# A two-layer hybrid block on one core: a fourth Strassen group per layer, with another sum, another order of the adding transfers, earlier bank copies and moved condition sums

## The chip, the cores and the metric

The kernel runs on one core of a Trainium2 chip. The metric is the device time in microseconds (us). The kernel before was run three times: 1801.11, 1798.59 and 1798.97 us, so its median is 1798.97 us. A further execution was profiled: it took 1799.28 us, and its recorded span, from the first to the last instruction, is 1797.2 us.

## The reference

Two layers are applied to one sequence of 512 tokens of width 1024, all in float32. Each layer has a mixing half (three attention-like branches, gated) and a convolutional feed-forward half. Both are preceded by an RMS norm whose scale and shift come from a condition vector. What matters here is the condition and the feed-forward half:

```
mod = silu(c) @ w_ada + b_ada                      # [6144] per layer
shift1, scale1, gate1, shift2, scale2, gate2 = jnp.split(mod, 6, axis=-1)
...                                                # mixing half, updates x
h2 = modulate(rms_norm(x, norm2_g), shift2, scale2)
u, g = jnp.split(h2 @ w_up, 2, axis=-1)            # w_up: 1024 x 5632, so u and g are 512 x 2816
u = causal_dwconv(u, w_conv, b_conv)               # 3 taps along the sequence
y = (jax.nn.silu(u) * g) @ w_down                  # 2816 x 1024
x = x + gate2 * y
```

## The kernel before, in words

**Weights.** The host cuts all weight matrices into 128x1024 float32 tiles (512 KB) in the order of use. Matrix work goes by *units*: one unit uses one such tile. A tile is loaded from DRAM by a transfer on SyncE's queue (`dma_to`) into one of six buffers (`wr`, `NR = 6`). ScalarE rounds it to the matmul's format (`prep_hi`, line 194, the tile `wh`), and VectorE subtracts that to get the rest (`prep_lo`, line 203, the tile `wl`). `wh` and `wl` have five buffers each. Activations are split in the same way (`hhi`, `hlo`), and every product is three matmuls: wh·hhi, wh·hlo, wl·hhi.

**Feed-forward up-projection.** `w_up` gives 22 columns (blocks of 128) of u and 22 of g, and column j of both is needed together. Per layer, columns 0 to 2 are made in `head_group`, beside the norm. Columns 3 to `J0 - 1` are made one after the other by `col_block`: one unit is one block of 24 matmuls over 512 tokens, first u, then g. Columns from `J0` on are made in *Strassen groups* of four columns (`ff_group`; with `NG = 3` groups, `J0` is 10).

**A group.** The four u columns and four g columns and the eight 128-wide slices of the input make a 2x2 by 2x2 block product over half the tokens each. It takes seven block products instead of eight. Each is two units of 24 matmuls over 256 tokens, so a group has 14 units. Four of the seven weight operands are sums of weight tiles. They are made before use by *adding transfers*: GpSimd issues a DMA that adds a tile from DRAM onto a tile that is in a buffer (`acc_to`, line 186). `_plan` lists the units, with "r" for a raw tile and the tile that is added to it, if any. In the order of products the operands are a11; a21+a22; a12; that sum + a11; a11+a21; the sum of the fourth product + a12; a22. `accs` is the list of adding transfers; `acc_to` takes them strictly from its front, and only when the buffer's earlier use is past.

The products accumulate in PSUM banks (bA, bB, bC, two halves t = 0 and 1). Between two products a bank's state is copied out or combined: `e1`, `e5`, `u2` (line 1175) and `c21` are copies by ScalarE, `c11`, `c22`, `c12` are sums by VectorE. `at(n, ...)` files such a step under the group's n-th unit. At each unit, `prod` first prepares the tiles of units ahead (`prep_lo` to the third unit, `prep_hi` to the fourth), and then issues the steps filed there. `u2` must be done before the fifth product goes on in bank bA.

**Sums of the input.** Four of the seven activation operands are sums too: per slice k, `t_sum` makes two sums (ta, tb) and rounds them, `t_low` makes the rests. They are issued one by one between the plain blocks (list `TS`).

**Condition sums.** `mod` is made on VectorE: a row block of `w_ada` (512 KB) is loaded by SyncE's queue into one of the six weight buffers (`ada_dma`, line 225) and multiplied with the condition and summed up in one instruction (`ada_sum`, line 230). There are 80 of these. Every second `tick`, of which each plain block has two, does one of them while `ada_on` is set; `ada_need` does what is still missing when a section is needed. While such jobs are left, `dma_to` keeps one weight buffer back.

Each engine and each queue works in the order of issue, which is the order of this program.

Of the kernel before, what the change touches and what calls it, by code (L numbers as in the profile page):

```python
# [53 lines left out]
NG = 3  # L54
# [8 lines left out]
def _plan():  # L63
# [28 lines left out]
def tile_hybrid_layers(ctx: ExitStack, tc: tile.TileContext, xT, cvec, wall, wada, par, a2, cst, tabs, out):  # L92
# [105 lines left out]
    def prep_lo(u):  # L198
        while state["lo"] < min(u, NU):
# [4 lines left out]
            wgt[i] = (hi, lo)  # L204
            state["lo"] += 1
# [238 lines left out]
    def head_group(l, sec, nm, h, half):  # L444
# [42 lines left out]
        else:  # L487
# [77 lines left out]
    def layer(l, nm, h):  # L565
# [517 lines left out]
        due = {}  # L1083
        acts = [None] * KFF
# [10 lines left out]
        def t_sum(k):  # L1095
            ta, tb = slot("ta"), slot("tb")
            c, d = tks.pop((l, k)), tks.pop((l, k + 4))
# [7 lines left out]
            ah, bh = slot("tah", F32R), slot("tbh", F32R)  # L1105
            A.copy(ah[:, H0], ta[:, H0])
            A.activation(ah[:, H1], ta[:, H1], AF.Identity, bias=tabd[:, 4 + k:5 + k])
            A.copy(bh, tb)
            tmid[k] = ta, tb, ah, bh

        def t_low(k):
            ta, tb, ah, bh = tmid.pop(k)
            al, bl = slot("tal", F32R), slot("tbl", F32R)
            V.tensor_tensor(al[:, H0], ta[:, H0], ah[:, H0].bitcast(F32), op=ALU.subtract)
            V.scalar_tensor_tensor(out=al[:, H1], in0=ta[:, H1], scalar=tabd[:, 4 + k:5 + k],
                                   in1=ah[:, H1].bitcast(F32), op0=ALU.add, op1=ALU.subtract)
            V.tensor_tensor(bl, tb, bh.bitcast(F32), op=ALU.subtract)
            tt[k, 1], tt[k, 2] = (ah, al, 0), (ah, al, 256)
# [435 lines left out]
```

## Time and profile before

| | us |
|---|---|
| median of 3 runs | 1798.97 |
| the profiled execution | 1799.28 |
| its span | 1797.2 |
| TensorE busy with matmuls | 1771.0 (99%) |
| VectorE busy | 1084.3 (60%) |
| ScalarE busy | 741.2 (41%) |
| GpSimd busy | 147.1 (8%) |
| layer 0: 14 plain blocks, from 577.36 | 76.17 |
| layer 0: three groups, 653.53 to 794.71 | 141.18 |
| layer 1: 14 plain blocks, from 1476.10 | 76.17 |
| layer 1: three groups, 1552.27 to 1673.22 | 120.95 |

Matmuls are pipelined, so the time of a stretch is read from the start of one matmul to the start of another, not from the durations. The last four rows are such distances; a plain block is thus 76.17/14 = 5.44 us, and a unit of a group in layer 1 is 120.95/42 = 2.88 us.

### The profile page before, as it was taken

What the parts mean: (1) busy time and instruction counts of PE and PEld (TensorE: products, weight loads), DVE (VectorE), ACT (ScalarE), POOL (GpSimd) and SP (SyncE); (2) the same over time, 40 slices, a digit from 0 to 9 for tenths busy, and PEclk for the clock granted to TensorE, in tenths of its full rate; (3) what the DMA queues carried; (4) which work ended last, traced back from release to release, by engine and by line L of the source; (5) the groups of instructions that cost most, each with busy time, mean ns of one, the idle gap of its engine ahead of it and who ended that gap; (6) DMA issues with size and microseconds to landing.
All of it is one profiled execution on the core that took longest, in us unless ns stands there. A gap on an engine that the chain in (4) does not pass through costs nothing.

```text
span 1797.2 us, 24309 instructions
## 1 busy us (share of the span) xinstructions
PE 1771.0 (99%) x9601; PEld 1518.8 (85%) x9601; DVE 1084.3 (60%) x1639; ACT 741.2 (41%) x1233; POOL 147.1 (8%) x191
## 2 busy tenths in 40 slices
PE   8999999999999989999999999999999999999999
PEld 6888778888888879988898887788888888999887
DVE  7767654565666766675555576545644467466731
ACT  3674433432324335563236544334323244355610
POOL 3221100000010011100001111000000100111000
PEclk9999999999999999999999999999999999999999
DMA  9342223456553468774622422334552334587431
GB/s 366 124 135 66 71 95 110 145 174 227 182 174 101 150 192 199 191 243 146 243 90 94 133 67 71 96 130 145 163 182 94 109 115 117 119 221 191 163 111 42
DMA packets 78510, 259.99 MB, mean 145 GB/s; under 512 B 9096, under 2 KB 9522, under 8 KB 78396
## 3 DMA queue, kind: packets, MB, share of 16 engines
q1 hardware_dynamic: 68748, 224.86, 36.8%
q0 software_dynamic: 9648, 33.58, 9.0%
q8 instruction: 75, 1.23, 0.3%
q14 instruction: 39, 0.32, 0.1%
HBM read 250.00 MB, written 8.40 MB: 144 GB/s over the span
## 4 chain that ended last, share of the span: by engine, by line
PE 82%; DVE 9%; DMA 3%; ACT 3%; issue 2%; SPq 0%; POOL 0%; ACTq 0%; DVEq 0%; POOLq 0%
PE bm L320 17%; PE bm L322 17%; PE bm L321 17%; PE bm L459 4%; PE ga L459 4%; PE bm L627 3%; PE bm L628 3%; PE bm L629 3%; PE bm L1158 3%; PE bm L1160 2%; PE bm L1161 2%; DMA wr<-wall 2%; ACT wh L194 1%; PE ba L1161 1%; PE ba L1160 1%
## 5 line engine op out<-in xcount | busy, mean ns | idle before, releaser
L203 DVE TENSOR_TENSOR wl<-wr,wh 128x1024 fp32r<-128x1024 f32 x338 | 412.3, 1223 | 293.1 <-ACT wh L194 292.1
L194 ACT CAST wh<-wr 128x1024 fp32r<-128x1024 f32 x338 | 351.2, 1046 | 286.2 <-PE bm L321 130.0
L320 PE MATMUL bm<-hhi,wh 128*128 128x512 f32 x912 | 366.1, 401 | 0.0
L322 PE MATMUL bm<-hhi,wl 128*128 128x512 f32 x912 | 355.7, 390 | 0.0
L321 PE MATMUL bm<-hlo,wh 128*128 128x512 f32 x912 | 355.5, 390 | 0.0
L320 PEld LDWEIGHTS bm<-hhi,wh 128*128 128x128 f32 x912 | 171.3, 188 | 37.1 <-issue 2.8
L322 PEld LDWEIGHTS bm<-hhi,wl 128*128 128x128 f32 x912 | 171.2, 188 | 36.8
L321 PEld LDWEIGHTS bm<-hlo,wh 128*128 128x128 f32 x912 | 171.5, 188 | 35.9 <-issue 1.4
L320 PE MATMUL bm<-fah,wh 128*128 128x512 f32 (+1 forms) x374 | 141.0, 377 | 0.0
L321 PE MATMUL bm<-fal,wh 128*128 128x512 f32 (+1 forms) x374 | 140.8, 377 | 0.0
L322 PE MATMUL bm<-fah,wl 128*128 128x512 f32 (+1 forms) x374 | 140.8, 377 | 0.0
L230 DVE SCALAR_TENSOR_TENSOR ar<-ar,cact 128x1024 f32<-128x1024 f32 x80 | 97.4, 1219 | 8.5 <-DMA ar<-wada 8.5
L627 PE MATMUL bm<-wh,hhi 128*128 128x512 f32 (+1 forms) x256 | 96.1, 376 | 0.0
L628 PE MATMUL bm<-wl,hhi 128*128 128x512 f32 (+1 forms) x256 | 93.5, 365 | 0.0
L629 PE MATMUL bm<-wh,hlo 128*128 128x512 f32 (+1 forms) x256 | 93.3, 365 | 0.0
L322 PEld LDWEIGHTS bm<-fah,wl 128*128 128x128 f32 x374 | 70.4, 188 | 13.0
L320 PEld LDWEIGHTS bm<-fah,wh 128*128 128x128 f32 x374 | 70.4, 188 | 12.8
L321 PEld LDWEIGHTS bm<-fal,wh 128*128 128x128 f32 x374 | 70.4, 188 | 12.7
L1022 DVE SCALAR_TENSOR_TENSOR x<-bm,mod,x 128x512 f32<-128x512 f32 (+1 forms) x39 | 25.3, 654 | 80.6 <-PE bm L322 80.5
L186 POOL DMA_DIRECT2D wr<-wall x48 | 41.7, 986 | 378.6 <-DVE wl L203 217.2
L985 ACT ACTIVATE mg<-bm,der 128x512 f32<-128x512 f32 x48 | 32.9, 685 | 73.7 <-PE bm L322 73.7
L1158 PE MATMUL bm<-tbh,wh 128*128 128x256 f32 x192 | 56.0, 292 | 6.4 <-ACT uu L1175 6.4
(288 smaller groups left out, 3431.5 us busy)
## 6 DMA issues: line engine op xcount, KB each, us to landing
wr<-wall SPq DMA_DIRECT2D x302, 512.0 KB, 3.6
ar<-wada SPq DMA_DIRECT2D x80, 512.0 KB, 4.2
wr<-wall POOLq DMA_DIRECT2D x48, 512.0 KB, 9.2
ad<-wada SPq DMA_DIRECT2D x32, 256.0 KB, 6.1
x<-xT SPq DMA_DIRECT2D x16, 256.0 KB, 4.8
x<-xm SPq DMA_DIRECT2D x16, 256.0 KB, 6.6
xm<-x POOLq DMA_DIRECT2D x10, 256.0 KB, 3.3
cumb<-cumd POOLq DMA_DIRECT2D x8, 256.0 KB, 6.3
```

What stands on the lines that cost most here:

```text
L194: A.copy(hi, raw[plan[i][1]])
L203: V.tensor_tensor(lo, raw[plan[i][1]], hi.bitcast(F32), op=ALU.subtract)
L230: V.scalar_tensor_tensor(out=r, in0=r, scalar=1.0, in1=cact, op0=ALU.mult, op1=ALU.mult, accum_out=mod[l][:, b:b + 1])
L320: T.matmul(o, lhsT=wh, rhs=ah, start=first, stop=False)
L321: T.matmul(o, lhsT=wh, rhs=al, start=False, stop=False)
L322: T.matmul(o, lhsT=wl, rhs=ah, start=False, stop=last)
L459: T.matmul(banks[f % GB][:, ts], lhsT=got[f // 8][wi][:, (f % 8) * 128:(f % 8) * 128 + 128], rhs=h[kc][hi][:, ts], start=kc == 0 and hf != ...
L627: T.matmul(o, lhsT=h[k][0][:, bs], rhs=wh[:, ws], start=k == 0, stop=False)
L628: T.matmul(o, lhsT=h[k][0][:, bs], rhs=wl[:, ws], start=False, stop=False)
L629: T.matmul(o, lhsT=h[k][1][:, bs], rhs=wh[:, ws], start=False, stop=k == KD - 1)
L1158: T.matmul(o, lhsT=wh[:, sl], rhs=ah, start=first and i == 0 and k == 0, stop=False, skip_group_check=True)
L1160: T.matmul(o, lhsT=wh[:, sl], rhs=al, start=False, stop=False, skip_group_check=True)
```

## The change

- `NG` is 4, so `J0` is 6: per layer, eight plain blocks are replaced by a fourth group of 14 units.
- The sixth product's operand (the sum of the fourth product + a12) is made by VectorE: when the fourth product's tile has been split, one instruction adds it onto a12 in a12's buffer ("v" in the plan). Three pairs of adding transfers per group are left of four.
- The list of adding transfers is sorted by when the buffer that they add to was last used.
- In `prod`, the steps that free or combine banks come first in a unit (`first_at`), ahead of the preparation, and `wl` is prepared one unit earlier, as far ahead as `wh`.
- `t_sum` and `t_low` are each cut in two (ta, tb). Five of the pieces move into `head_group`, two into the first group, and the others stay between the plain blocks, up to two behind each.
- No condition sums run between the plain blocks: `ada_on` is cleared before them and not after.

```diff
-NG = 3
+NG = 4
...
-        for dst, src in ((a11, None), (a21, a22), (a12, None), (a21, a11), (a11, a21), (a21, a12), (a22, None)):
+        for op, dst, src in (("r", a11, a11), ("r", a21, a22), ("r", a12, a12), ("r", a21, a11), ("r", a11, a21),
+                             ("v", a12, a21), ("r", a22, a22)):
             for i in range(2):
-                v.append(("r", dst[i], None if src is None else src[i]))
+                v.append((op, dst[i], src[i] if src != dst else None))
...
+    sums = {}
     for i, t in enumerate(plan):
-        if t[2] is not None:
+        if t[0] == "v":
+            sums[last[t[2]]] = t[1], t[2]
+        elif t[2] is not None:
             accs.append((i, t[1], t[2], last.get(t[1], -1)))
         endv[t[1]] = last[t[1]] = i
+    accs.sort(key=lambda a: a[3] if a[3] >= 0 else a[0] - 6.5)
...
             V.tensor_tensor(lo, raw[plan[i][1]], hi.bitcast(F32), op=ALU.subtract)
             wgt[i] = (hi, lo)
+            if i in sums:
+                d, a = sums[i]
+                V.tensor_tensor(raw[d], raw[d], raw[a], op=ALU.add)
...
+                for f in extra.get(kc, ()) if extra else ():
+                    f()
...
-        TS = [lambda: t_sum(0), lambda: t_low(0), lambda: t_sum(1), lambda: t_low(1),
-              lambda: t_sum(2), lambda: t_low(2), lambda: t_sum(3), lambda: t_low(3)]
+        TS = [lambda k=k, f=f: f(k) for k, f in ((0, ta_sum), (1, ta_sum), (0, ta_low), (2, ta_sum), (1, ta_low),
+                                                 (3, ta_sum), (2, ta_low), (0, tb_sum), (3, ta_low), (1, tb_sum),
+                                                 (0, tb_low), (2, tb_sum), (1, tb_low), (3, tb_sum))]
+        TL = [lambda k=k, f=f: f(k) for k, f in ((2, tb_low), (3, tb_low))]
+        ex = {kc: [TS.pop(0)] for kc in range(3, KD)}
...
                 for t in range(2):
-                    prep_lo(cur[0] + 3)
-                    prep_hi(cur[0] + 4)
+                    for f in early.pop(cur[0], []):
+                        f()
+                    prep_to(cur[0] + 4)
                     dma_to(cur[0] + 12, True)
...
+            for n in range(len(TL)):
+                at(1 + n, TL.pop(0))
             for t in range(2):
-                at(1 + t, e1, t)
-                at(3 + t, e5, t)
-                at(5 + t, c11, t)
-                at(7 + t, u2, t)
-                at(9 + t, c22, t)
-                at(11 + t, c12, t)
-                at(13 + t, c21, t)
+                first_at(1 + t, e1, t)
+                first_at(3 + t, e5, t)
+                first_at(5 + t, c11, t)
+                first_at(7 + t, u2, t)
+                first_at(9 + t, c22, t)
+                first_at(11 + t, c12, t)
+                first_at(13 + t, c21, t)
...
+        ada_on[0] = False
+        while ada_raw:
+            i, b, post, r = ada_raw.pop(0)
+            ada_sum(i, b, r)
+            if post:
+                post()
         free(NA)
         far[0] = 6
         for j in range(3, J0):
...
             col_block(h2, pu_evac)
-            if TS:
-                TS.pop(0)()
+            for f in TS[:2]:
+                f()
+            del TS[:2]
             col_block(h2, pg_evac)
-            if TS:
-                TS.pop(0)()
-        ada_on[0] = False
+            for f in TS[:2]:
+                f()
+            del TS[:2]
         far[0] = 12
-        while ada_raw:
-            i, b, post, r = ada_raw.pop(0)
-            ada_sum(i, b, r)
-            if post:
-                post()
```

Three places show how the instructions move. In the listings a name's number is the tile's, L is the line in the kernel that the listing is of, so line 203 before is line 208 now, 1065 to 1077 are 1075 to 1087, 1175 is 1202, and 186 is 191.

**VectorE between the plain blocks, layer 0, before.** `wl` is the rest of a weight tile, `fu` the convolution's taps and the gate of one column, `ar` a condition sum, `ta` and `tb` the input sums.

```order
L203 TENSOR_TENSOR wl_5126<-wr_4934,wh_5124 128x1024
L1065 SCALAR_TENSOR_TENSOR fu_5143<-bm_5039,par0_85,fu_5143 128x511
L1067 SCALAR_TENSOR_TENSOR fu_5143<-bm_5039,par0_85,fu_5143 128x510
L1077 TENSOR_TENSOR fu_5143<-fu_5143,bm_5091 128x512
L230 SCALAR_TENSOR_TENSOR ar_5117,mod1_88<-ar_5117,cact_93 128x1024
L1098 TENSOR_TENSOR ta_5164<-ht_4641 128x256
L1099 SCALAR_TENSOR_TENSOR ta_5164<-ht_4813,ta_5164 128x256
L1101 SCALAR_TENSOR_TENSOR tb_5165<-ht_4813,tabd_4629,ht_4641 128x256
L1103 TENSOR_TENSOR tb_5165<-ht_4813 128x256
L1104 TENSOR_TENSOR tb_5165<-tb_5165,ta_5164 128x256
L203 TENSOR_TENSOR wl_5178<-wr_4998,wh_5176 128x1024
L230 SCALAR_TENSOR_TENSOR ar_5162,mod1_88<-ar_5162,cact_93 128x1024
```

The same place now:

```order
L208 TENSOR_TENSOR wl_5061<-wr_4955,wh_5059 128x1024
L1075 SCALAR_TENSOR_TENSOR fu_5078<-bm_4965,par0_85,fu_5078 128x511
L1077 SCALAR_TENSOR_TENSOR fu_5078<-bm_4965,par0_85,fu_5078 128x510
L1087 TENSOR_TENSOR fu_5078<-fu_5078,bm_5025 128x512
L1128 SCALAR_TENSOR_TENSOR tb_5096<-ht_4791,tabd_4629,ht_4638 128x256
L1130 TENSOR_TENSOR tb_5096<-ht_4791 128x256
L1131 TENSOR_TENSOR tb_5096<-tb_5096,ta_4847 128x256
L1138 TENSOR_TENSOR tbl_5102<-tb_5050,tbh_5051 128x512
L208 TENSOR_TENSOR wl_5106<-wr_4961,wh_5104 128x1024
```

The condition sums are gone from between the blocks, and a piece that needs ScalarE's rounding (`tbl`) now stands behind the sums of the next slice.

**ScalarE around `u2` in the first group, before.** `wh` is a rounded weight tile; `wr_5272` and `wr_5312` hold the operand of the sixth product here, the one that the fourth adding transfer makes.

```order
L194 CAST wh_5671<-wr_5312 128x1024
L1169 COPY gg_5673<-ba_5538 128x2x256
L194 CAST wh_5702<-wr_5353 128x1024
L194 CAST wh_5731<-wr_5387 128x1024
L194 CAST wh_5763<-wr_5272 128x1024
L1175 COPY uu_5578<-bm_5535 128x2x256
L194 CAST wh_5795<-wr_5312 128x1024
L1175 COPY uu_5610<-bm_5536 128x2x256
```

The same place now; the sixth product's operand is in `wr_5023` and `wr_5063`, a12's buffers:

```order
L199 CAST wh_5354<-wr_4959 128x1024
L199 CAST wh_5386<-wr_4961 128x1024
L199 CAST wh_5417<-wr_4963 128x1024
L1202 COPY uu_5255<-bm_5220 128x2x256
L199 CAST wh_5449<-wr_5023 128x1024
L1202 COPY uu_5287<-bm_5221 128x2x256
L199 CAST wh_5481<-wr_5063 128x1024
```

`u2` has moved ahead of the rounding of the sixth product's tiles, and those tiles no longer come from a transfer.

**GpSimd's adding transfers of the first group, before**, from the second pair on: a21 += a11 twice, a11 += a21 twice, a21 += a12 twice. The names in brackets are the counters that GpSimd waits on: DMASW those of earlier adding transfers, DMAHW those of loads, DVE and Activation those of VectorE and ScalarE.

```order
L186 DMA wr_5272<-wall 128x1024 [waits DMASW2_49,DMASW0_49,DVE_49]
L186 DMA wr_5312<-wall 128x1024 [waits DMASW3_49,DMASW1_49,DVE_49]
L186 DMA wr_5353<-wall 128x1024 [waits DMAHW4_49,DMAHW5_49,DMAHW1_49,DMASW4_49]
L186 DMA wr_5387<-wall 128x1024 [waits DMAHW6_49,DMAHW5_49,DMASW5_49]
L186 DMA wr_5272<-wall 128x1024 [waits DMASW6_49,DMASW2_49,DVE_49]
L186 DMA wr_5312<-wall 128x1024 [waits DMASW7_49,DMASW3_49,DVE_49]
```

The first group's transfers now, from the first pair on (a21 += a22, a11 += a21, a21 += a11):

```order
L191 DMA wr_4957<-wall 128x1024 [waits DMAHW4_49,DMAHW1_49,DMAHW5_49,DMAHW0_49,DMAHW7_49,DMASW0_49,DVE_49]
L191 DMA wr_4959<-wall 128x1024 [waits DMAHW2_49,DMAHW5_49,DMAHW0_49,DMAHW6_49,DMASW1_49,DVE_49]
L191 DMA wr_4961<-wall 128x1024 [waits DMAHW3_49,DMASW2_49,DVE_49]
L191 DMA wr_4963<-wall 128x1024 [waits DMAHW4_49,DMAHW6_49,DMASW3_49,DVE_49]
L191 DMA wr_4957<-wall 128x1024 [waits DMASW4_49,DMASW0_49,DVE_49]
L191 DMA wr_4959<-wall 128x1024 [waits DMASW5_49,DMASW1_49,DVE_49]
```

And VectorE now at the end of the fourth product's tiles (`wr_4957`, `wr_4959`), with the two new sums:

```order
L208 TENSOR_TENSOR wl_5323<-wr_4957,wh_5321 128x1024
L212 TENSOR_TENSOR wr_5023<-wr_5023,wr_4957 128x1024
L208 TENSOR_TENSOR wl_5356<-wr_4959,wh_5354 128x1024
L212 TENSOR_TENSOR wr_5063<-wr_5063,wr_4959 128x1024
L1199 TENSOR_TENSOR uu_5255<-uu_5255,bm_5224 128x2x256
```

The sum for a11 now stands ahead of the second sum for a21, and the fourth pair of transfers has become two VectorE instructions ahead of `c11` (line 1199).

By the order of issue, the 80 condition sums fall as follows. Before: 34 in layer 0 ahead of the feed-forward half, 15 between its plain blocks, 13 in its down-projection, 18 in layer 1's mixing half. Now: 34, 1 (ahead of the plain blocks), 13 and 32.

More of the change, by code (lines that the diff above doesn't have):

```diff
@@ L442, in ada0_sum, with head_group @@
         ada0_fin(kc, i, ada0_part(kc, i), E)
-    def head_group(l, sec, nm, h, half):
+    def head_group(l, sec, nm, h, half, extra=()):
         live[0] += NA
@@ L1083, in layer @@
         due = {}
+        early = {}
         acts = [None] * KFF
@@ L1093, in layer, with ta_sum @@
         tmid = {}
[L1095 to L1097 removed]
+        def ta_sum(k):
+            ta, ah = slot("ta"), slot("tah", F32R)
+            c, d = tks[l, k], tks[l, k + 4]
             V.tensor_tensor(ta[:, H0], c[:, H0], c[:, H1], op=ALU.subtract)
@@ L1100, in t_sum, with ta_low, tb_sum @@
                                    op1=ALU.subtract)
+            A.copy(ah[:, H0], ta[:, H0])
+            A.activation(ah[:, H1], ta[:, H1], AF.Identity, bias=tabd[:, 4 + k:5 + k])
+            tmid[k] = ta, ah
+        def ta_low(k):
+            ta, ah = tmid[k]
+            al = slot("tal", F32R)
+            V.tensor_tensor(al[:, H0], ta[:, H0], ah[:, H0].bitcast(F32), op=ALU.subtract)
+            V.scalar_tensor_tensor(out=al[:, H1], in0=ta[:, H1], scalar=tabd[:, 4 + k:5 + k],
+                                   in1=ah[:, H1].bitcast(F32), op0=ALU.add, op1=ALU.subtract)
+            tt[k, 1], tt[k, 2] = (ah, al, 0), (ah, al, 256)
+        def tb_sum(k):
+            tb, bh = slot("tb"), slot("tbh", F32R)
+            ta, _ = tmid[k]
+            c, d = tks.pop((l, k)), tks.pop((l, k + 4))
             V.scalar_tensor_tensor(out=tb[:, H0], in0=d[:, H1], scalar=tabd[:, k:k + 1], in1=c[:, H1], op0=ALU.add,
@@ L1104, in t_sum, with tb_low @@
             V.tensor_tensor(tb[:, H1], tb[:, H1], ta[:, H0], op=ALU.add)
-            ah, bh = slot("tah", F32R), slot("tbh", F32R)
-            A.copy(ah[:, H0], ta[:, H0])
-            A.activation(ah[:, H1], ta[:, H1], AF.Identity, bias=tabd[:, 4 + k:5 + k])
             A.copy(bh, tb)
[L1109 to L1116, printed above, removed]
+            tmid[k] = tb, bh
+        def tb_low(k):
+            tb, bh = tmid.pop(k)
+            bl = slot("tbl", F32R)
             V.tensor_tensor(bl, tb, bh.bitcast(F32), op=ALU.subtract)
-            tt[k, 1], tt[k, 2] = (ah, al, 0), (ah, al, 256)
             tt[k, 3], tt[k, 4] = (bh, bl, 0), (bh, bl, 256)
-        TS = [lambda: t_sum(0), lambda: t_low(0), lambda: t_sum(1), lambda: t_low(1),
-              lambda: t_sum(2), lambda: t_low(2), lambda: t_sum(3), lambda: t_low(3)]
+        TS = [lambda k=k, f=f: f(k) for k, f in ((0, ta_sum), (1, ta_sum), (0, ta_low), (2, ta_sum), (1, ta_low),
[3 more added lines that the diff above has]
+        ex = {kc: [TS.pop(0)] for kc in range(3, KD)}
         def ff_group(j0):
@@ L1142, in at, with first_at @@
                 due.setdefault(base + n, []).append(lambda: f(*a))
+            def first_at(n, f, *a):
+                early.setdefault(base + n, []).append(lambda: f(*a))
             def prod(banks, key, first):
                 for t in range(2):
-                    prep_lo(cur[0] + 3)
-                    prep_hi(cur[0] + 4)
+                    for f in early.pop(cur[0], []):
+                        f()
+                    prep_to(cur[0] + 4)
                     dma_to(cur[0] + 12, True)
@@ L1231, in ff_group @@
             free(3)
-        fb = head_group(l, 3, nm2, h2, True)
+        fb = head_group(l, 3, nm2, h2, True, ex)
         ahead()
@@ L1265, in layer @@
         tt.clear()
+        for n, fs in early.items():
+            due[n] = fs + due.get(n, [])
+        early.clear()
         rest = [f for n in sorted(due) for f in due[n]]
```

## The prediction

> **What bounds the kernel now.** I read the page first, then the busy table of the feed-forward stretches of both layers, then TensorE's waits.
>
> ```profile
> span 1797.2 us, 24309 instructions
> PE 1771.0 (99%) x9601; PEld 1518.8 (85%) x9601; DVE 1084.3 (60%) x1639; ACT 741.2 (41%) x1233; POOL 147.1 (8%) x191
> ```
>
> TensorE is busy throughout; the others have room on average. So time is won only by fewer or faster matmuls, or from the few places where TensorE stands. These are the plain blocks and the three groups of layer 0, then the same of layer 1:
>
> ```profile
> core 0: us, PE busy (x) PEld busy (x) DVE busy (x) ACT busy (x) POOL busy (x), PEclk, DMA share, GB/s
> 577.36:653.53 76.17, 76.17 (x338) 63.08 (x336) 55.70 (x90) 29.29 (x41) 1.83 (x2) 1.00 0.49 154
> 653.53:794.71 141.18, 129.24 (x1009) 127.84 (x1008) 92.27 (x109) 72.12 (x95) 19.13 (x22) 0.94 0.78 200
> 1476.10:1552.27 76.17, 76.17 (x338) 63.06 (x336) 48.99 (x74) 33.43 (x47) 2.65 (x3) 1.00 0.35 94
> 1552.27:1673.22 120.95, 120.95 (x1009) 120.95 (x1008) 81.25 (x92) 68.95 (x89) 18.06 (x21) 1.00 0.81 204
> ```
>
> The reader is to see that the same 1008 matmuls take 141.18 us in layer 0 and 120.95 us in layer 1, where TensorE never stands and its granted clock is 1.00. Layer 0 loses 20.23 us. TensorE's waits with a line of the groups are these (us in total, times, longest), and all seven lie in layer 0:
>
> ```profile
> PE bm L1158 <- ACT uu L1175: 6.4, 4, 3.4
> PE bm L1158 <- DVE fu L1067: 3.0, 1, 3.0
> PE ba L1158 <- ACT wh L194: 1.8, 1, 1.8
> PE ba L1161 <- DVE wl L203: 0.8, 1, 0.8
> ```
>
> That is 12.0 us of standing. The rest is the clock, 0.94 on the mean. After the longest wait the matmuls come every 0.2136 us (22 of them from the first to the second row here) instead of 120.95/1008 = 0.1200:
>
> ```profile
> 691.03 0.41 PE L1161 MATMUL bm<-tbh,wl 128*128 128x256 f32 x1
> 695.73 0.41 PE L1158 MATMUL bm<-tbh,wh 128*128 128x256 f32 x1
> ```
>
> A mean of 0.94 over 141.18 us means 16.9 us at half clock; each such microsecond does 0.1200/0.2136 of the work, so 7.4 us are lost. 12.0 + 7.4 = 19.4 of the 20.23; restarts are the remainder.
>
> Two causes show. First, `u2` (line 1175) stands on ScalarE behind a rounding that waits for an adding transfer, and TensorE waits for `u2`:
>
> ```profile
> 688.86 1.04 ACT L194 CAST wh<-wr 128x1024 fp32r<-128x1024 f32 x1 [2.95 <-DMA wr<-wall]
> 689.81 0.58 ACT L1175 COPY uu<-bm 128x512 f32<-128x512 f32 x1
> 690.44 0.58 PE L1158 MATMUL bm<-tbh,wh 128*128 128x256 f32 x1 [3.43 <-ACT uu L1175]
> ```
>
> By the order of issue that rounding is the sixth product's tile, the fourth adding transfer. Second, condition loads (line 225) stand in SyncE's queue, and each holds a weight buffer. Four of them come in a row just as layer 0's groups start, and the next two weight loads, a12 of the first group by the order of issue, start 10.8 us and more into the group; in layer 1 the second of the same pair started 22.6 us ahead of it:
>
> ```profile
> 651.89 5.29 SPq L225 DMA_DIRECT2D ar<-wada  x3
> 662.02 0.33 SPq L225 DMA_DIRECT2D ar<-wada  x1
> 664.30 2.74 SPq L180 DMA_DIRECT2D wr<-wall  x2
> 1529.65 0.33 SPq L180 DMA_DIRECT2D wr<-wall  x1
> ```
>
> Layer 1 runs the same code without condition sums there, so it is a control for that half of the change.
>
> **The change, part by part.**
>
> *Fourth group.* Per layer eight plain blocks go, 8/14 x 76.17 = 43.53 us, and a group comes at layer 1's pace, 120.95/3 = 40.32 us: a gain of 3.21 us per layer, 6.42 in all. Seven products instead of eight would give an eighth, 5.4 us; the row gives less, because a 256-token matmul takes 0.1200 us and not half of 76.17/336 = 0.2267. [...] The trace says 0.1200 and 0.2267, so the 3.21 stands.
>
> The six added units per layer cost ScalarE and VectorE a split each:
>
> ```profile
> L203 DVE TENSOR_TENSOR wl<-wr,wh 128x1024 fp32r<-128x1024 f32 x338 | 412.3, 1223 | 293.1 <-ACT wh L194 292.1
> L194 ACT CAST wh<-wr 128x1024 fp32r<-128x1024 f32 x338 | 351.2, 1046 | 286.2 <-PE bm L321 130.0
> L186 POOL DMA_DIRECT2D wr<-wall x48 | 41.7, 986 | 378.6 <-DVE wl L203 217.2
> L230 DVE SCALAR_TENSOR_TENSOR ar<-ar,cact 128x1024 f32<-128x1024 f32 x80 | 97.4, 1219 | 8.5 <-DMA ar<-wada 8.5
> ```
>
> 12 x 1.22 = 14.7 us of VectorE and 12 x 1.05 = 12.6 of ScalarE, beside TensorE: in layer 1's groups VectorE is busy 81.25 of 120.95 and ScalarE 68.95. On the path: nothing. If the cover goes, the late tile's 1.05 + 1.22 us show at once.
>
> *Sum by VectorE.* 16 instructions of the shape of line 203 (two SBUF operands, 128x1024): 16 x 1.22 = 19.6 us of VectorE. A group's VectorE work goes from 81.25/3 = 27.1 to 29.5 us, of 40.32: hidden. Behind each sum wait the next rests and `c11`; a unit is 2.88 us and the rests run three units ahead, so 1.22 us late is covered. GpSimd's transfers stay 48 (eight groups of six), so its 41.7 us stay; per group it is a quarter less, and the weight bytes per unit fall from 16 tiles in 14 units to 14 in 14.
>
> *Bank copies first.* `u2` no longer follows the sixth product's rounding, and that tile comes from VectorE. What is left behind `u2` is that rounding: it waits for `u2`, which waits for the fourth product, but is wanted only three units, 8.6 us, later. This takes out the 6.4 us and its clock.
>
> *Order of the adding transfers.* The a11 transfer no longer stands behind a21's second one, which waits for later rests. From issue to use one takes about 7.0 us (GpSimd's start of one in layer 1 to the rounding that ended its wait on it):
>
> ```profile
> 1561.30 0.85 POOL L186 DMA_DIRECT2D wr<-wall  x1 [4.06 <-DVE wl L203]
> 1568.34 1.05 ACT L194 CAST wh<-wr 128x1024 fp32r<-128x1024 f32 x1 [1.93 <-DMA wr<-wall]
> ```
>
> The rests are now made three units ahead, so a21's second transfer starts some five units, 14 us, ahead of its use: no cost, and the 1.93 us wait should shrink. A gain only off the path.
>
> *No condition sums beside the plain blocks.* 14 of layer 0's sums move into layer 1's mixing half, which then carries 32. Whether that costs is shown by the two mixing halves now (VectorE's condition sums, two records each, then all engines):
>
> ```profile
> 288.00:577.36 289.36, 41.68 (x68) 1.00 0.49 166
> 1186.74:1476.10 289.36, 20.84 (x34) 1.00 0.42 139
> 288.00:577.36 289.36, 289.32 (x1470) 246.64 (x1469) 173.24 (x271) 98.99 (x183) 11.49 (x17) 1.00 0.49 166
> 1186.74:1476.10 289.36, 289.34 (x1470) 246.63 (x1469) 153.78 (x236) 98.96 (x183) 11.49 (x17) 1.00 0.42 139
> ```
>
> 34 sums in layer 0 and 17 in layer 1 take the same 289.36 us. So 32 cost nothing. In layer 0's down-projection 13 remain, as before, and 34 + 1 + 13 = 48 is just what is wanted by then (32 of layer 0, 16 of layer 1's shift and scale): no spare one, but none missing.
>
> *Six plain blocks instead of fourteen, and the moved input sums.* Here the cover shrinks, and this is where I look for a loss. In layer 1 ScalarE and VectorE run behind TensorE after `head_group` and need about 10.2 us per column (pair of blocks, 10.88 us of TensorE), gate to gate:
>
> ```profile
> 1495.69 0.69 DVE L1077 TENSOR_TENSOR fu<-fu,bm 128x512 f32<-128x512 f32 x1 [0.76 <-ACT fu L1071]
> 1515.45 0.63 ACT L1071 ACTIVATE fu<-fu 128x512 f32<-128x512 f32 x1 [3.64 <-DVE fu L1067]
> 1516.12 0.69 DVE L1077 TENSOR_TENSOR fu<-fu,bm 128x512 f32<-128x512 f32 x1 [0.76 <-ACT fu L1071]
> ```
>
> The last two rows are the third column, the last plain one now. Its silu starts at 1515.45, while the groups would start at 1476.10 + 6 x 5.44 = 1508.74. The group's fourth tile is split behind that silu: 1515.45 + 0.63, then 1.05 and 1.22, ready at 1518.4. TensorE wants its rest at 1508.74 + 3 x 2.88 + 2 x 0.12 = 1517.6. So the upper bound is 0.8 us per layer. The lower bound: the new order gives each column one slice's input sums as now, but with ScalarE's rounding further ahead of its use; a wait of VectorE for ScalarE of up to 1 us per column falls away, and the tile is 2 us early. I take zero, since nearly all of the interval lies there.
>
> **The sum.** 1799.28 (the profiled execution) - 20.23 - 6.42 = 1772.63 us. That execution is 0.31 us above the median of the three, less than their spread, so I give 1772.6 for the median.
>
> **Rivals.**
>
> *Short stalls of the first groups.* If the fourth tile is late by 0.8 us and the input sums shift a few more, each layer pays 1 to 3 us, plus clock. [...]
>
> With half clock for as much as one of the two causes had (7.4/2 = 3.7) each layer pays up to 6: 1775 to 1785.
>
> *The first group is late for want of plain blocks, not for the condition loads.* Then only `u2`'s part of layer 0 is won, and both layers pay 3.0 + 1.8 + 0.8 = 5.6 us and, by their share of the first 9.0 us of waits, 4.6 of clock: 1772.6 + 2 x 10.2 = 1793. Against it: layer 1's third column is done when 0.8 us are missing at most, and a12's second load started 22.6 us early there.
>
> *VectorE becomes the bound, and the kernel slower.* The sum, `c11` and the rests stand in one queue; if `c11`, now ahead of the rests, waits for its bank while tiles three units on are wanted, every group stalls. One wait as the longest seen, 3.43 us, with half of the 7.4 us of clock, in each of eight groups: 1772.6 + 8 x 7.1 = 1829. It is slower only from (26.65 + 3.6)/8 = 3.8 us per group on. Against it: 29.5 of 40.32 us.
>
> *The moved sums show after all,* 14 x 1.22 = 17.1 us in layer 1's mixing half: 1790. Against it: the equal 289.36.
>
> **Chances.** The sum 0.68, short stalls 0.16, the late first group 0.08, moved sums 0.02, VectorE 0.04, and 0.02 for losses that just cancel the gain. 0.2% is 3.6 us and about what can be told from no change; faster by more: 0.68 + 0.16 + 0.08 + 0.02 = 0.94, within 0.02, slower 0.04. For 8 in 10 the range takes the sum and the short stalls: from 1770 (2.6 us under the sum, about the spread of the runs) to 1784.
>
> **What would show it.** Right: the two stretches from the first plain block to the last group's end are 6 x 5.44 + 56 x 2.88 = 193.9 us in each layer, with clock 1.00; no wait of line 1158's successor on `u2`; no condition sum between the plain blocks and 32 in layer 1's mixing half, still 289.4 us long; fewer and shorter waits of ScalarE's rounding on transfers. Wrong: a wait on `wl` or `wh` in the first three units of the first group, a clock below 1.00 behind it, or waits on `c11` in every group.

## The result, and the profile after

| | before | after |
|---|---|---|
| median, us (range, runs) | 1799.25 (1798.59 to 1801.11, 4) | 1772.85 (1772.09 to 1773.08, 4) |
| the profiled execution, us | 1799.28 | 1772.72 |
| ratio of the times | | 0.9851, 95% interval 0.9834 to 0.9868 |
| layer 0: plain blocks + groups, us | 76.17 + 141.18 = 217.35 | 32.64 + 161.27 = 193.91 |
| layer 1: the same | 76.17 + 120.95 = 197.12 | 32.64 + 161.27 = 193.91 |

The change saves 26.40 us on the medians and 26.56 between the two profiled executions. The two stretches account for it: 217.35 - 193.91 = 23.44 in layer 0 and 197.12 - 193.91 = 3.21 in layer 1, 26.65 in all.

The head of the page after, and the busy table of the stretches (layer 0's plain blocks and groups, then layer 1's):

```profile
span 1770.9 us, 24972 instructions
...
PE 1757.4 (99%) x9889; PEld 1521.2 (86%) x9889; DVE 1123.2 (63%) x1679; ACT 759.6 (43%) x1261; POOL 147.2 (8%) x191
```

```profile
core 0: us, PE busy (x) PEld busy (x) DVE busy (x) ACT busy (x) POOL busy (x), PEclk, DMA share, GB/s
577.71:610.35 32.64, 32.64 (x145) 27.03 (x144) 23.45 (x39) 13.71 (x19) 2.66 (x4) 1.00 0.55 123
610.35:771.62 161.27, 161.27 (x1345) 161.26 (x1344) 122.25 (x136) 93.82 (x122) 17.27 (x20) 1.00 0.70 178
1453.03:1485.67 32.64, 32.64 (x145) 27.03 (x144) 23.47 (x39) 13.70 (x19) 1.69 (x2) 1.00 0.48 107
1485.67:1646.94 161.27, 161.27 (x1345) 161.27 (x1344) 122.25 (x136) 93.81 (x122) 17.07 (x20) 1.00 0.70 178
```

Layer 0 and layer 1 are now alike to 0.01 us, TensorE is busy in all of both and its clock is 1.00. 161.27/4 = 40.32 us is the pace of a group that layer 1 had before. The list of TensorE's waits has no line of the groups any more (the first of its six; the others are 2.4 us and less, all from outside the groups):

```profile
PE fT L771 <- DVE st L839: 2.5, 2, 1.3
...
```

The weight tiles' groups of instructions, to be held against lines 203 and 194 before, and the new sums:

```profile
L208 DVE TENSOR_TENSOR wl<-wr,wh 128x1024 fp32r<-128x1024 f32 x350 | 426.5, 1223 | 274.0 <-ACT wh L199 273.3 <-DMA wr<-wall 0.2
L199 ACT CAST wh<-wr 128x1024 fp32r<-128x1024 f32 x350 | 362.8, 1047 | 221.2 <-PE bm L329 121.3 <-DMA wr<-wall 52.2 <-issue 38.9
...
L212 DVE TENSOR_TENSOR wr<-wr 128x1024 f32<-128x1024 f32 x16 | 19.5, 1219 | 0.0
```

Twelve more splits and 16 sums of 1.22 us. ScalarE's rounding waits 52.2 us for weight transfers in all, where the list of ScalarE's waits before has 84.7.

The place where the prediction looked for a loss is the first group of layer 0. These rows are ScalarE's third silu and its rounding of the group's fourth tile, VectorE's rest of that tile, and TensorE's first matmul with it:

```profile
614.86 0.63 ACT L1081 ACTIVATE fu<-fu 128x512 f32<-128x512 f32 x1 [2.12 <-DVE fu L1077]
615.39 1.03 ACT L199 CAST wh<-wr 128x1024 fp32r<-128x1024 f32 x1
616.46 1.23 DVE L208 TENSOR_TENSOR wl<-wr,wh 128x1024 fp32r<-128x1024 f32 x1 [0.25 <-ACT wh L199]
619.22 0.28 PE L1188 MATMUL ba<-tah,wl 128*128 128x256 f32 x1
```

The rest is done at 616.46 + 1.23 = 617.69, 1.53 us before TensorE takes it. The mixing half of layer 1 with its moved condition sums is as long as before: from the last group of layer 0 to the first plain block of layer 1 it is 1453.03 - 771.62 = 681.41 us, and it was 1476.10 - 794.71 = 681.39.

```profile
1163.67:1453.03 289.36, 38.00 (x62) 1.00 0.49 164
```

That row is VectorE's condition sums in the 289.36 us ahead of layer 1's plain blocks: 31 of them (two records each) where 17 stood, and TensorE does not show it.

### The profile page after: what moved, and what is told of

It is laid out like the page before. It is cut to its first block, busy times and chain, and to the rows that moved or that the text cites. A ratio compares the mean times of both kernels' runs of the same rounds, so it can differ in the third digit from the quotient of the medians.

```text
span 1770.9 us, 24972 instructions
## 1 busy us (share of the span) xinstructions
PE 1757.4 (99%) x9889; PEld 1521.2 (86%) x9889; DVE 1123.2 (63%) x1679; ACT 759.6 (43%) x1261; POOL 147.2 (8%) x191
## 4 chain that ended last, share of the span: by engine, by line
PE 90%; DVE 6%; ACT 2%; issue 1%; DMA 0%; SPq 0%; POOL 0%; ACTq 0%; DVEq 0%
PE bm L328 17%; PE bm L330 17%; PE bm L329 17%; PE bm L467 4%; PE bm L1188 4%; PE bm L1187 4%; PE bm L1185 4%; PE ga L467 4%; PE bm L637 3%; PE bm L638 3%; PE bm L639 3%; PE ba L1188 2%; PE ba L1187 2%; PE ba L1185 2%; DVE fl L761 1%; ACT wh L199 1%
## 5 line engine op out<-in xcount | busy, mean ns | idle before, releaser
L208 DVE TENSOR_TENSOR wl<-wr,wh 128x1024 fp32r<-128x1024 f32 x350 | 426.5, 1223 | 274.0 <-ACT wh L199 273.3
L328 PE MATMUL bm<-hhi,wh 128*128 128x512 f32 x784 | 316.3, 403 | 0.0
L330 PE MATMUL bm<-hhi,wl 128*128 128x512 f32 x784 | 306.0, 390 | 0.0
L329 PE MATMUL bm<-hlo,wh 128*128 128x512 f32 x784 | 305.7, 390 | 0.0
L328 PEld LDWEIGHTS bm<-hhi,wh 128*128 128x128 f32 x784 | 147.3, 188 | 32.0 <-issue 2.8
L330 PEld LDWEIGHTS bm<-hhi,wl 128*128 128x128 f32 x784 | 147.1, 188 | 32.0
L329 PEld LDWEIGHTS bm<-hlo,wh 128*128 128x128 f32 x784 | 147.4, 188 | 30.9 <-issue 1.4
L329 PEld LDWEIGHTS bm<-fal,wh 128*128 128x128 f32 x374 | 70.4, 188 | 12.8
L328 PEld LDWEIGHTS bm<-fah,wh 128*128 128x128 f32 x374 | 70.4, 188 | 12.8
L1185 PE MATMUL bm<-tbh,wh 128*128 128x256 f32 x256 | 72.4, 283 | 0.0
L1187 PE MATMUL bm<-tbl,wh 128*128 128x256 f32 x256 | 72.4, 283 | 0.0
L1188 PE MATMUL bm<-tbh,wl 128*128 128x256 f32 x256 | 72.4, 283 | 0.0
```

Source lines behind the costliest of these rows:

```text
L208: V.tensor_tensor(lo, raw[plan[i][1]], hi.bitcast(F32), op=ALU.subtract)
L328: T.matmul(o, lhsT=wh, rhs=ah, start=first, stop=False)
L329: T.matmul(o, lhsT=wh, rhs=al, start=False, stop=False)
L330: T.matmul(o, lhsT=wl, rhs=ah, start=False, stop=last)
L1185: T.matmul(o, lhsT=wh[:, sl], rhs=ah, start=first and i == 0 and k == 0, stop=False, skip_group_check=True)
L1187: T.matmul(o, lhsT=wh[:, sl], rhs=al, start=False, stop=False, skip_group_check=True)
```

## The experiments

The time came out as predicted, so the question is which of the six edits made it, and by what. A run is given by its median, its range, and the ratio of its time to that of the kernel before run beside it, with a 95% interval. "Loses" is said of a layer's groups against 120.95 us for three and 161.27 for four, the times without a wait. A tile is late when TensorE stands waiting for it. Line numbers are those of the kernel that a row is of.

### The condition sums alone, on the kernel before (b_cond)

```diff
+        ada_on[0] = False
+        while ada_raw:
+            ...
         free(NA)
         far[0] = 6
...
-        ada_on[0] = False
         far[0] = 12
-        while ada_raw:
-            ...
```

> The kernel before with one edit: no condition sums between the plain blocks (three groups, old copies, old sums). If the condition loads are the root of all that layer 0's groups lose, as layer 1 suggests, layer 0's three groups take 121.0 us like layer 1's, and the time falls by 20.2 us to about 1779. If the bank copy behind the fourth adding transfer is a cause of its own, its waits (6.4 us) and half of the clock's 7.4 us stay, and the time is about 1789.

1783.02 us (1778.82 to 1785.44), ratio 0.9912, 0.9890 to 0.9934. In the profiled execution, 1778.82 us, layer 0's groups have nothing left to lose:

```profile
653.21:774.16 120.95, 120.95 (x1009) 120.95 (x1008) 81.42 (x92) 68.73 (x89) 18.29 (x21) 1.00 0.81 205
```

So in this execution the edit by itself wins back all 20.23 us there, the wait on `u2` included, although `u2` stands where it stood and the fourth adding transfer is still there. It is the shortest of four. The other three took 3.6 to 6.6 us more, and there is no trace of them: where they lost it is open. By the medians the edit is worth 1799.24 - 1783.02 = 16.2 us.

### The condition sums put back into the kernel after (a_cond)

```diff
         far[0] = 12
+        ada_on[0] = False
+        while ada_raw:
+            ...
         flush()
...
-        ada_on[0] = False
-        while ada_raw:
-            ...
         free(NA)
```

> The changed kernel with one edit undone: condition sums run between the plain blocks again (six of them, in layer 0 only). If the condition loads are the root and the other edits do not cover it, layer 0's first group is late again, by 5 to 12 us: 1778 to 1785. If the copies first and the sum by VectorE suffice, it stays at 1773 to 1775.

1781.95 us (1781.67 to 1782.94), ratio 0.9909, 0.9892 to 0.9926. Layer 0's groups, then the two waits of TensorE:

```profile
610.17:780.86 170.69, 165.03 (x1345) 164.12 (x1344) 129.78 (x149) 94.93 (x124) 18.16 (x21) 0.98 0.71 183
PE ba L1185 <- ACT wh L199: 4.4, 2, 2.7
PE ba L1188 <- DVE wl L208: 1.2, 2, 0.8
```

It loses 9.42 us in layer 0 and 0.01 in layer 1. The price of the condition sums is thus 20.2 us in the kernel before, where 15 of them ran beside 14 blocks, and 9.4 in the new one, where the trace has seven beside six. Late first tiles remain, the wait on `u2` does not come back.

The trace also says what costs the time here. In the whole execution VectorE waits 0.1 us ahead of its condition sums, where it waited 8.5 us for their loads before. These are its line for them, then the last of the seven, the third silu behind the taps that follow it, and TensorE's wait for the tile that is rounded behind that silu:

```profile
L238 DVE SCALAR_TENSOR_TENSOR ar<-ar,cact 128x1024 f32<-128x1024 f32 x80 | 97.3, 1218 | 0.1
...
620.29 1.22 DVE L238 SCALAR_TENSOR_TENSOR ar<-ar,cact 128x1024 f32<-128x1024 f32 x1
623.06 0.63 ACT L1081 ACTIVATE fu<-fu 128x512 f32<-128x512 f32 x1 [4.61 <-DVE fu L1077]
624.67 0.58 PE L1185 MATMUL ba<-tah,wh 128*128 128x256 f32 x1 [2.70 <-ACT wh L199]
```

In the kernel before, the first wait in the groups goes back to a condition load: VectorE's sum waits for it, and the taps stand behind the sum.

```profile
655.59 1.23 DVE L230 SCALAR_TENSOR_TENSOR ar<-ar,cact 128x1024 f32<-128x1024 f32 x1 [2.59 <-DMA ar<-wada]
659.56 0.55 PE L1158 MATMUL bm<-hhi,wh 128*128 128x256 f32 x1 [3.00 <-DVE fu L1067]
```

So a few instructions of 1.22 us in VectorE's queue are enough to make the first tiles late, and waiting for loads came on top in the kernel before. No run keeps the sums and takes away their loads, so how the 20.2 us divide between the two is not shown.

### Bank copies first alone, on the kernel before (b_first)

```diff
-                    prep_lo(cur[0] + 3)
-                    prep_hi(cur[0] + 4)
+                    for f in early.pop(cur[0], []):
+                        f()
+                    prep_to(cur[0] + 4)
                     dma_to(cur[0] + 12, True)
...
-                at(7 + t, u2, t)
+                first_at(7 + t, u2, t)
```

(and so for the other six steps). The rests are made one unit earlier with it.

> The kernel before with one edit: in a group's units the bank steps come first and the rests one unit earlier. If the bank copy behind a rounding is a cause of its own, the waits on u2 (6.4 us) and some of the clock go: 1788 to 1791. If the late weight loads are the root, the copy no longer waits, but the tile behind it is late all the same, and TensorE waits for that: 1795 to 1799.

1791.63 us (1790.18 to 1794.75), ratio 0.9961, 0.9949 to 0.9973. TensorE's waits in its groups:

```profile
PE ba L1163 <- ACT wh L194: 3.7, 1, 3.7
...
PE bm L1166 <- DVE wl L203: 1.5, 2, 0.8
...
```

The waits on `u2` went from 6.4 us to 0.4 and layer 0's loss from 20.23 to 9.88. But waits for late weight tiles came in their place (3.7, 1.5 and another 1.0 us), and layer 1, which had lost nothing, now loses 1.60 us (122.55). With the old transfers this edit is thus not free.

### The fourth group alone, on the kernel before (b_ng4), and with the condition sums moved (b_ng4_cond)

```diff
-NG = 3
+NG = 4
...
+        while TS:
+            TS.pop(0)()
         flush()
```

Six plain blocks leave room for six of the eight input sums; the last two stand in one piece ahead of the first group.

> The kernel before with four groups and nothing else (what is left of the input sums runs ahead of the first group). Per layer 3.2 us fewer matmul time. If the other edits only mend what the condition loads spoil, layer 1 gains its 3.2 us and layer 0 still loses 15 to 25 us: 1790 to 1800. If six plain blocks are too few without the other edits, layer 1 stands too, 3 to 10 us: 1797 to 1810.

1809.01 us (1804.84 to 1811.14), ratio 1.0055, 1.0037 to 1.0073: slower than before. Layer 0 takes 32.64 + 184.76 and loses 23.49, layer 1 takes 32.64 + 172.50 and loses 11.23. Of these 34.7 us, seven waits on `u2` make 12.8, waits for weight tiles of the first groups 6.6 and waits for the last input sums 3.3, 22.7 together. The other 12.0 us are not divided further: the granted clock of this execution is 0.991 on the mean, where the kernel after has 0.999, and in a_v3 a restart takes 0.15 to 0.16 us more than its wait.

> The kernel before with four groups and no condition sums between the plain blocks, and nothing else. In the run with four groups alone, layer 1, which has no condition sums there, took 205.1 us from the first plain block to the last group's end, 11.2 us over the 193.9 us without waits. If that is for want of plain blocks, layer 0 now loses the same 11 us: 1772.6 + 2 x 11.2 = 1795. If it came from the adding transfers of layer 0 or from elsewhere, layer 1 loses less: 1773 to 1785.

1800.42 us (1794.51 to 1803.37), ratio 0.9998, 0.9983 to 1.0013: no change. The profiled execution is one of the short ones, 1795.51; layer 0's groups lose 171.21 - 161.27 = 9.94 us, layer 1's 174.00 - 161.27 = 12.73. Its waits, then VectorE and ScalarE in layer 0 from the last of the two input sums that stand in one piece (silu, rounding and rests of the group's fourth and fifth tile):

```profile
PE bm L1158 <- ACT uu L1175: 6.8, 4, 2.4
PE ba L1158 <- ACT wh L194: 3.9, 2, 2.1
...
PE ba L1161 <- DVE wl L203: 1.2, 2, 0.8
```

```profile
617.47 0.69 DVE L1117 TENSOR_TENSOR tbl<-tb,tbh 128x512 fp32r<-128x512 f32 x1
...
619.77 0.63 ACT L1071 ACTIVATE fu<-fu 128x512 f32<-128x512 f32 x1 [1.66 <-DVE fu L1067]
620.30 1.98 ACT L194 CAST wh<-wr 128x1024 fp32r<-128x1024 f32 x2
621.36 2.36 DVE L203 TENSOR_TENSOR wl<-wr,wh 128x1024 fp32r<-128x1024 f32 x2 [0.25 <-ACT wh L194]
```

The same tile is rounded at 615.39 in the kernel after. So fewer plain blocks, with two input sums in one piece ahead of the first group, do make that group late, in both layers and without any condition sum beside them, and `u2` waits return in both layers too. Something among the other edits takes away both.

### One edit at a time out of the kernel after (a_dma4, a_late, a_unsorted)

The fourth sum by an adding transfer again:

```diff
-                             ("v", a12, a21), ("r", a22, a22)):
+                             ("r", a21, a12), ("r", a22, a22)):
```

> The changed kernel with the sixth product's operand made by a fourth adding transfer again (copies first, sorted). If the sum by VectorE is what takes the stalls away, waits of TensorE come back in the groups, 1 to 4 us each where a rounding waits for that transfer: 1778 to 1795. If the copies first suffice, the rounding's wait is hidden by its three units: 1773 to 1775.

Bank steps last in the unit and rests one unit later, as before:

```diff
+                    prep_lo(cur[0] + 3)
+                    prep_hi(cur[0] + 4)
+                    dma_to(cur[0] + 12, True)
                     for f in early.pop(cur[0], []):
                         f()
-                    prep_to(cur[0] + 4)
-                    dma_to(cur[0] + 12, True)
```

> The changed kernel with the bank steps behind the preparation again and the rests one unit later (sum by VectorE, sorted). If the sum by VectorE is the cure, no rounding ahead of u2 waits for long and it stays at 1773 to 1775. If the order of the copies is, waits on u2 come back: 1778 to 1790.

The adding transfers in the old order:

```diff
-    accs.sort(key=lambda a: a[3] if a[3] >= 0 else a[0] - 6.5)
```

> The changed kernel with the adding transfers in the old order of use (sum by VectorE, copies first). By the prediction the order is worth nothing on the path: 1772 to 1774. If the transfer for a11 is late behind the second one for a21, the fifth product's tiles are late by up to the 3 us that separate two of them, in each of eight groups: up to 1795.

| | median, us (range) | ratio, 95% interval | layer 0, layer 1, us |
|---|---|---|---|
| a_dma4 | 1773.41 (1772.89 to 1773.64) | 0.9852, 0.9837 to 0.9867 | 193.91, 193.91 |
| a_late | 1773.70 (1773.29 to 1774.92) | 0.9855, 0.9838 to 0.9871 | 193.91, 193.92 |
| a_unsorted | 1774.29 (1773.97 to 1774.96) | 0.9858, 0.9843 to 0.9873 | 193.90, 195.01 |

None of the three is needed while the other two stand. Only the old order of the transfers shows a trace of its own, one wait of 0.8 us on a rest in layer 1, which costs 1.10 us there.

### All three out at once (a_tonly)

The three diffs above together. Of the change remain the fourth group, the cut and moved input sums and the moved condition sums.

> The kernel after, but with the fourth sum by an adding transfer, the old order of the adding transfers, and bank steps last and rests one unit later: of the change remain the fourth group, the cut and moved input sums and the moved condition sums. Theory (the moved input sums alone are the cover): 1773 to 1776 us, 193.9 us in each layer, at most single waits under 1 us. Rival (one of the three taken out must stand): as in the kernel before with four groups and moved condition sums, 203 to 207 us per layer, so 1793 to 1800 us, waits on uu and on wh.

1797.29 us (1790.99 to 1800.25), ratio 0.9978, 0.9967 to 0.9989. My theory that the input sums alone do it fell. TensorE's one kind of wait in the groups, the groups of both layers, and ScalarE at `u2` of the first group:

```profile
PE bm L1185 <- ACT uu L1202: 14.0, 11, 2.8
```

```profile
611.16:782.83 171.67, 163.31 (x1346) 161.68 (x1344) 113.75 (x130) 95.14 (x124) 26.10 (x30) 1.00 0.79 195
1497.14:1668.09 170.95, 165.29 (x1345) 164.50 (x1344) 113.73 (x130) 95.07 (x124) 25.77 (x30) 0.98 0.80 196
```

```profile
635.61 1.04 ACT L198 CAST wh<-wr 128x1024 fp32r<-128x1024 f32 x1 [1.87 <-DMA wr<-wall]
636.56 0.58 ACT L1202 COPY uu<-bm 128x512 f32<-128x512 f32 x1
```

Two things are told apart here. No wait on a first tile is left, so the moved input sums do cover those. But eleven times, in seven of the eight groups, TensorE waits for `u2`, which stands on ScalarE right behind the rounding of a weight tile, and in ten of the eleven that rounding has itself waited for a transfer, as in the rows above. It is the prediction's first cause, and in this kernel no condition sum stands near it. Against it the VectorE sum, the sorted transfers and the early copies are three covers of which any two suffice. Whether one alone would was not tried.

### The input sums back between the plain blocks (a_ts)

```diff
-        ex = {kc: [TS.pop(0)] for kc in range(3, KD)}
+        ex = {}
...
-            for f in TS[:2]:
+            for f in TS[:3]:
```

> The kernel after, but none of the input sums' pieces in head_group: all 14 stand between the plain blocks, up to three behind each. Theory (the pieces moved into the head are what keeps the first group's tiles in time): five more pieces of about 0.8 us of VectorE each, 4 us, come ahead of the third column's gate; in the trace of after the first late tile is 1.3 to 1.5 us early, so it is 2.5 us late now in each layer, and with some clock behind it each layer loses 2.5 to 6 us: 1778 to 1785 us, waits on wh or wl in the first group of both layers. Rival (sorted transfers, VectorE's sum or early bank copies are the cover): no waits, 1773 us.

1779.87 us (1779.79 to 1780.19), ratio 0.9888, 0.9874 to 0.9902. The groups take 164.78 us in each layer, 3.51 more than after; 2 x 3.51 = 7.02 us, and the medians differ by 7.02. TensorE's waits there, all in the first group of each layer:

```profile
PE ba L1188 <- DVE wl L208: 3.0, 4, 0.8
...
PE ba L1185 <- ACT wh L199: 1.9, 4, 0.8
```

The place of the input sums is thus a cover of its own: with sorted transfers, VectorE's sum and early copies all in place, the first tiles are late again as soon as five more pieces stand ahead of the third column's gate.

### Three groups (a_ng3)

```diff
-NG = 4
+NG = 3
```

> The kernel after with three groups and 14 plain blocks per layer. Theory (each fourth group is worth 8 plain blocks less 14 units, 3.21 us, with nothing else lost or won): 1772.9 + 6.4 = 1779.3 us, 197.1 us from the first plain block to the last group's end in each layer. Rival (the fourth group costs something that three do not, as buffers or late tiles): under 1778 or over 1781.

1779.22 us (1778.90 to 1780.13), ratio 0.9885, 0.9872 to 0.9898. The stretches are 76.16 + 120.96 = 197.12 and 76.16 + 120.95 = 197.11 us, without a wait, 3.21 and 3.20 us above four groups; the medians differ by 6.37.

### VectorE's sum three times as long (a_v3)

```diff
                 V.tensor_tensor(raw[d], raw[d], raw[a], op=ALU.add)
+                for _ in range(2):
+                    V.tensor_tensor(raw[d], raw[d], raw[d], op=ALU.max)
```

> The kernel after; behind each of VectorE's 16 weight sums stand two more instructions of its size (the maximum of the tile with itself), 2.44 us more in the queue at each, 39 us in all. Theory (VectorE has room of some 10 us per group, and its rests run three units, 8.6 us, ahead): 1773 to 1775 us, no or single waits in the groups. Rival (VectorE is close to the bound there, the sum stands in the way of rests and bank steps): waits on wl or on a bank in every group, 8 x 2 x 1 to 2.4 us, 1789 to 1812 us.

1801.98 us (1800.49 to 1804.80), ratio 1.0015, 1.0006 to 1.0023. The room that I had read off was not there: 39 us more of VectorE's work cost 29 us. TensorE's waits, which fall into groups 2 to 4 of both layers:

```profile
PE bm L1190 <- DVE wl L208: 16.7, 12, 2.3
PE bm L1187 <- ACT wh L199: 4.1, 6, 1.2
```

The third group of layer 0 shows the way. First the kernel after: ScalarE's copy `e5` (line 1196), VectorE's rest of the eighth tile, TensorE's first use of it, then the ninth tile's rest and its use:

```profile
707.76 0.59 ACT L1196 COPY gg<-ba 128x512 f32<-128x512 f32 x1 [3.16 <-DVE fu L1228]
709.33 1.23 DVE L208 TENSOR_TENSOR wl<-wr,wh 128x1024 fp32r<-128x1024 f32 x1 [1.66 <-ACT wh L199]
711.38 0.28 PE L1188 MATMUL bm<-tah,wl 128*128 128x256 f32 x1
712.21 1.22 DVE L208 TENSOR_TENSOR wl<-wr,wh 128x1024 fp32r<-128x1024 f32 x1
714.26 0.28 PE L1188 MATMUL bm<-tbh,wl 128*128 128x256 f32 x1
```

Then the same place with the longer sums, from VectorE's last two gating products of the group before (line 1230) on:

```profile
714.41 1.29 DVE L1230 TENSOR_TENSOR fu<-fu,gg 128x512 f32<-128x512 f32 x2
715.79 0.59 ACT L1198 COPY gg<-ba 128x512 f32<-128x512 f32 x1 [5.68 <-DVE fu L1230]
717.35 1.22 DVE L208 TENSOR_TENSOR wl<-wr,wh 128x1024 fp32r<-128x1024 f32 x1 [1.65 <-ACT wh L199]
718.63 0.39 PE L1190 MATMUL bm<-tah,wl 128*128 128x256 f32 x1 [0.76 <-DVE wl L208]
724.02 0.39 PE L1190 MATMUL bm<-tbh,wl 128*128 128x256 f32 x1 [2.26 <-DVE wl L208]
```

`e5` writes into a buffer whose last tile, a `gg` of the group before, is still needed for its gating, and ScalarE's next rounding stands behind `e5`. So the two engines take turns: VectorE's sum, its gating, ScalarE's `e5`, the rounding, the rest. In the kernel after the eighth tile's rest is ready at 709.33 + 1.23 = 710.56 and wanted at 711.38, 0.82 us later; the ninth's is ready at 713.43 and wanted at 714.26, 0.83 later. Two sums that are each 2.44 us longer make 4.88 us, less 0.83 is 4.05. TensorE lost 0.71 + 0.91 + 2.42 = 4.04 us at this place (distances from the matmul ahead of each wait, less 0.12). Each of them is 0.15 to 0.16 us longer than the wait itself. The six groups lose 23.7 us so. The other 6.1 us of the stretches' 29.8 go with the clock, which is 0.996 on the mean in this execution and 0.999 in the kernel after, and with the second matmul behind each wait: the one behind the last row comes 0.22 us later, where 0.12 is the pace. How they divide is not shown. The lead is the same, 0.82 to 0.84 us, in all six of these groups of the kernel after. In a_dma4, which has no such sum, the same two rests are 1.98 and 3.12 us early.

## Why the prediction was right, step by step

*The sum.* 1772.63 us were predicted for the profiled execution, and it took 1772.72. Both stretches are 193.91 us where 193.9 was written, with clock 1.00. That it fits to 0.1 us is in part luck: two terms were put at zero, and the steps on VectorE's sum and on the six plain blocks below show how little was between them and a loss.

*Fourth group.* Right: 3.21 us per layer by a_ng3, which takes away that alone. The pace it rests on is in the trace after too: 161.27/1344 = 0.1200 us for each 256-token matmul, as in the kernel before.

*Layer 0's loss.* The size was right, and the naming was half right. The prediction called the `u2` wait and the condition loads two causes, each with its edit. With three groups one of the two edits was enough in the execution that was traced: b_cond clears both kinds of wait without touching `u2`, so there the `u2` wait was a consequence of the condition sums. The earlier copies do take the `u2` wait away by themselves, as predicted, and 20.23 - 9.88 = 10.35 us of layer 0 with it (b_first). `u2` is a cause of its own with four groups, where a_tonly shows 14.0 us of it without a condition sum nearby. So the edits that the prediction credited with part of the 20 us win nothing over b_cond's profiled execution; they keep the fourth group from costing more than it brings (b_ng4_cond: 1800.42). The median of b_cond is 3.8 us above that of a_ng3, which has them all with three groups; so in its longer executions they may win something too, which is not shown. And for the second cause the prediction pointed at the late loads of a12, the group's fifth and sixth tile. TensorE waits at neither of these two units; the first waits go back to VectorE's queue, as the rows under a_cond show.

*Sum by VectorE.* Right that it costs nothing, wrong on how much room it has, and this is the step that would have failed first. The prediction read the room from the busy share (29.5 of 40.32 us) and from the rests' lead of three units, 8.6 us. That lead is one in the order of issue, not in time: in groups 2 to 4 the rests of the eighth and ninth tile are 0.82 and 0.83 us early, because VectorE's gating and ScalarE's `e5` bind the two queues together, and the sums take over half of what was there (1.98 and 3.12 us in a_dma4). It was luck that enough was left. The rival "VectorE becomes the bound" was priced as a wait of the bank steps in all eight groups; a_v3 shows the real form, late rests in six groups. It starts after 0.8 us of delay, and a loss of 29.8/6 = 5.0 us in each of the six was enough to eat the whole gain, where the rival had put the limit at 3.8 in each of eight.

*Bank copies first, and the order of the transfers.* The copies were credited with the 6.4 us of `u2` waits and their clock, the order with nothing on the path. Taken out of the kernel after, one at a time, both are worth next to nothing (a_late: +0.85 us in the median and no wait; a_unsorted: +1.44 us and one wait of 0.8), since the other covers stand. What the prediction did not say: copies first is not free by itself. On the kernel before it makes rests late and layer 1 loses 1.60 us (b_first).

*Condition sums in the other half.* Right: 681.41 us against 681.39.

*Six plain blocks.* Taken as zero between 2 us early and 0.8 us late; the fourth tile is 1.53 us early. It is so only because pieces of the input sums moved into the head: without that each layer loses 3.51 us (a_ts). The rival of the late first group, held at 0.08, therefore has a true mechanism. Its argument against ("layer 1's third column is done when 0.8 us are missing at most") was read from a kernel in which the last input sums stood behind the third column; with six blocks and the old order they stand ahead of the first group's tiles, and both layers lose about what the rival said, 9.94 and 12.73 us where it said 10.2, though part of that is the `u2` wait that it had left out.

## What to carry to other kernels

An engine's busy share is not its room at a place (here VectorE is busy 122.25 of 161.27 us, and its rests are 0.82 us early): take the time from the moment an operand is ready to the moment it is used, in the tightest repetition, and check it by making the added work two or three times as long. Blocks that are replaced were also cover for what stood beside them; a faster block brings its gain only when that work is moved as well, and a change that is slower alone (1809.01) can be worth 6.4 us with its covers. Where several safeguards come in one change, take them out one by one and then all together: here none of three was needed by itself, and without all three the gain was nearly gone.

## What the runs showed of the hardware

Equal waits did not cost equal clock. In a_v3 five waits of TensorE on the ninth tile are 2.25 or 2.26 us long and come at the same place of a group. The first five rows are the 4.46 us behind each of them. The last row is at the sixth place, behind a wait of 1.22 us on the eighth tile (columns as in the tables of stretches; the clock is the third number from the end):

```profile
677.86:682.32 4.46, 4.46 (x24) 4.46 (x25) 4.14 (x5) 0.70 (x2) 0.60 (x1) 0.62 0.68 183
724.02:728.48 4.46, 4.46 (x37) 4.46 (x38) 4.46 (x5) 1.34 (x2) 0.00 (x0) 1.00 0.65 174
768.68:773.14 4.46, 4.46 (x37) 4.46 (x38) 4.46 (x5) 2.38 (x3) 0.00 (x0) 1.00 0.67 183
1567.71:1572.17 4.46, 4.46 (x37) 4.46 (x38) 4.46 (x5) 1.34 (x2) 0.39 (x1) 1.00 0.68 170
1657.68:1662.14 4.46, 4.46 (x24) 4.46 (x25) 4.46 (x5) 1.58 (x3) 0.00 (x0) 0.62 0.72 189
1606.39:1610.85 4.46, 3.71 (x17) 3.50 (x18) 4.39 (x4) 3.27 (x4) 0.00 (x0) 0.62 0.25 44
```

Behind two of the five, the clock is 0.62 on the mean and 24 matmuls start instead of 37. In the kernel before, the clock's mean is 0.85 in the 33.20 us ahead of the 3.43 us wait, where the longest wait is one of 3.00 us, and 0.50 in 5 us behind it, where the matmuls come every 0.2136 us:

```profile
653.53:686.73 33.20, 27.68 (x193) 27.09 (x191) 20.90 (x27) 11.91 (x16) 5.21 (x6) 0.85 0.78 203
691.00:696.00 5.00, 5.00 (x26) 5.00 (x25) 1.42 (x3) 2.72 (x4) 1.73 (x2) 0.50 0.84 223
```

If the clock in a_v3 was either 1.00 or 0.50, a mean of 0.62 is a spell of 2 x 0.38 x 4.46 = 3.4 us at half clock, an estimate. It cost about (37 - 24) x 0.12 = 1.6 us. Behind three, nothing.

So the clock fell behind two of five waits of 2.25 or 2.26 us, and at the sixth place behind 1.22 us with another 0.76 us soon after it. On the mean the five waits cost 2/5 x 1.6 = 0.6 us on top of themselves, an estimate from this one execution. What decides whether the clock falls is not shown.

Whether this is also why some kernels spread more between runs than others is not shown, since one execution of each was traced. a_tonly, with waits up to 2.8 us, goes from 1790.99 to 1800.25; but a_cond, with waits up to 2.7 us, spreads by 1.27 us only, and b_cond, whose trace has no wait in the groups, by 6.6.
